# A hybrid attention and convolution trunk on one core: hi parts of late weight chunks cast from memory, their splits moved, a third partial-sum buffer

## The chip, the cores and the metric

The kernel runs on one core of one Trainium2 chip. The metric is device time in microseconds (us) of one execution. Before the change it is 522.34 us, the median of 3 runs (521.39 to 524.71).

A core has five engines, each with its own instruction queue worked strictly in order: TensorE (PE) does matmuls and transposes, VectorE (DVE) and ScalarE (ACT) do elementwise work, GpSimd (POOL) does elementwise work on SBUF and issues the DMAs that convert or accumulate, SyncE (SP) issues the plain DMAs. An instruction that waits for a semaphore holds up everything behind it in its engine's queue.

## The reference, cut to what matters

Two residual layers over x of 512 tokens by 1024 channels, in float32.

```python
def fox_moba_layer(x, norm_g, w_in, ..., w_out):          # layer 0
    proj = rms_norm(x, norm_g) @ w_in                     # 1024 x 4104
    ...                                                   # two kinds of attention, 8 heads each
    return x + (mix * jax.nn.silu(gate)) @ w_out

def conformer_conv_layer(x, norm_g, w_in, conv_w, conv_b, ln_g, ln_b, w_out):   # layer 1
    val, glu_gate, z = jnp.split(rms_norm(x, norm_g) @ w_in, 3, axis=-1)
    u = val * jax.nn.sigmoid(glu_gate)
    u = depthwise_causal_conv(u, conv_w, width=31) + conv_b
    u = jax.nn.silu(layer_norm(u, ln_g, ln_b)) * jax.nn.silu(z)
    return x + u @ w_out
```

The change lies in layer 1, and in how its weights are brought in.

## The kernel before, in words

**Weights.** All weights come as 36 chunks of 1024 rows by 256 columns (two of layer 0 by 260; 1 MB each; 0 to 15 are layer 0's input projection, 16 to 19 its output projection, 20 to 27 the GLU's value and gate columns in turn, 28 to 31 the z columns, 32 to 35 layer 1's output projection). A matmul is made as three products of rounded parts: hi*hi, hi*lo and lo*hi, where hi is the value rounded to the fp32r format and lo the rest. So each chunk is **split**: `load_w` (L152, issued by SP) loads it into a staging tile `wst`, of which there are two; `split_w` makes hi and lo. For chunks from 20 on, lo is made by ACT (L175: minus the rounded chunk) followed by a DMA that POOL issues and that adds the staged chunk onto it (L179). For the chunks in `CAST` (22, 26, 27, 28, 30, 31, 33, 34, 35) hi is made by a DMA that POOL issues and that converts the staged chunk (L169); for the others ACT does it (L173). Chunk 32 alone has its hi cast from memory (L1051) and its lo made by L160 and L161. A staging tile is free, and the load of the chunk after next can start, when the DMA of L179 has landed. hi and lo live in rings: `main` (whi and wlo, two each) or `wx` (four tiles, two chunks). `ahead(n)` traces all splits below n that have not been traced yet.

**Layer 1.** For each of 8 channel tiles ct (128 channels) `glu` makes u; the convolution's 31 taps are shared: DVE adds some of them up in a PSUM accumulator (L766), ACT multiplies the others into one of six `tm` tiles (L775; its first goes straight into the partial sum, L772), and POOL adds those to the partial sum `pacc` (L776). `conv_final` (L783, DVE) joins both sums, `conv_out` transposes the result on PE (L796), takes its statistics on DVE (L798) and puts it back by token on ACT (L799, `ctok`). `pacc` has two buffers, so a tile's ACT and POOL taps can begin when the tile two before it has been transposed. Tiles 6 and 7 are done in two halves of 256 tokens. The first half's taps of both are traced together, then `z_chunk` for chunks 28 to 30, with a split after each.

**The stretch that is written out.** From `conv_out(6, ...)` on, the order on PE, DVE, ACT and POOL is the order of the code (`manual_schedule`); elsewhere a scheduler sets it. The first half goes: transposes of tile 6, the z matmuls of tile 6, transposes of tile 7, most of the z matmuls of tile 7; `norm_stats(0)` (layer norm: variance on DVE, L904, its power of minus a half on POOL, L905, called lnr); `norm_cols` (L911, DVE); transposes back to channels (`ng_t`, L922); then, for four pairs p of channel tiles, `ng_s` (swish, ACT, L928, in the tiles `c`), `ng_m` (times z, DVE, L933), `ng_u` (hi, ACT, L936), `ng_l` (lo, DVE, L939), and the matmuls of four output units with chunks 33 and 34 (L361). The second half's taps of tiles 6 and 7 are put between these by the tables AQ (ACT and POOL) and DQ (DVE). After them the units of chunk 32 and 35 follow, with the second half's transposes between, and at last the same for the second half of the tokens.

Of the kernel before, what the change touches and what calls it, by code (L numbers as in the profile page):

```python
# [9 lines left out]
F32 = mybir.dt.float32  # L10
# [4 lines left out]
ALU = mybir.AluOpType  # L15
# [34 lines left out]
Z6 = 8  # L50
ZK = 6
AQ = (4, 0, 7, 1, 0, 1, 2, 1, 3, 3, 2, 1, 6, 0)
DQ = (3, 5, 2, 0, 0, 2, 2, 2, 4, 3, 3, 5, 99)
# [20 lines left out]
NLATE = 2  # L74
CB = 3
LATE1 = 0
# [18 lines left out]
def tile_kernel(ctx: ExitStack, tc: tile.TileContext, x, xt, w, small0, small1, l1_norm, out):  # L95
# [59 lines left out]
    def split_w(w, ring, eng, parts, cast):  # L155
        st, n = w
        if ring == "late":
# [10 lines left out]
        if cast:  # L168
            G.dma_start(hi, st)  # L169
        for k in range(0, KC, m):  # L170
# [56 lines left out]
    def fetch(i):  # L227
        if i < len(wsrc):
            raw[i] = load_w(*wsrc[i], 4 if i == 0 else 1)

# [517 lines left out]
    def conv_steps(ct, acc, pacc, n0, n):  # L748
# [20 lines left out]
        def astep(i):  # L769
            v, w = tap(i)  # L770
            if i == nv:
                A.activation(pacc[:, o], v, AF.Copy, scale=w)  # L772
                return
            tm = l1.tile([P, S], F32, tag="tm", name="tm", bufs=TMB)
            A.activation(tm[:, :n], v, AF.Copy, scale=w)  # L775
            G.tensor_tensor(pacc[:, o], pacc[:, o], tm[:, :n], op=ALU.add)  # L776

# [24 lines left out]
    def new_pacc():  # L802
        return l1.tile([P, S], F32, tag="pacc", name="pacc", bufs=2)

# [109 lines left out]

    pts_, cs_ = {}, {}

# [8 lines left out]
    def ng_s(h, k):  # L925
        pt = pts_[h, k // 2]
        c = cs_[h, k] = l1.tile([P, HT], F32, tag="c", name="c", bufs=CB)
        A.activation(c, pt[:, (k % 2) * HT:(k % 2 + 1) * HT], AF.Silu, bias=lnb[:, k:k + 1],  # L928
                     scale=lng[:, k:k + 1])
# [26 lines left out]
    for i in range(max(len(v6), len(v7) + LAG)):  # L956
        j = i - LAG
        for f in v6[i:i + 1] + (v7[j:j + 1] if j >= 0 else []):
            f()
    for i in range(max(len(a6), len(a7) + LAGA)):  # L960
        j = i - LAGA
        for f in a6[i:i + 1] + (a7[j:j + 1] if j >= 0 else []):
            f()
    for ct in late:
        conv_final(*ends[ct], 0, HT)()
    for c in range(3):
        z_chunk(28 + c, c)
        ahead(34 + c)

# [43 lines left out]
    with tc.manual_schedule(engines=engs):  # L1013
# [19 lines left out]
        for p in range(4):  # L1033
# [21 lines left out]
            for (c, t), po in zip(units, banks):  # L1055
                out1_mm(c, t, po, (2 * p, 2 * p + 1))
        for (c, t), po in zip(units, banks):
            out1_add(c, t, po)
# [129 lines left out]
```

## Time and profile before

| | before |
|---|---|
| median of 3 runs | 522.34 us |
| the profiled execution's own time | 522.39 us |
| its span, first to last instruction | 520.6 us |
| PE busy | 503.7 us, 97% |
| DVE, ACT, POOL busy | 373.0, 329.1, 232.6 us |
| mean granted TensorE clock | 0.996 |

The profiled execution took 0.05 us more than the median, and 1.8 us of its time lie outside the span. The page gives busy time, idle time and what ended it, by engine and line; a matmul's recorded time includes its way through the array, so that records overlap, and a PE that is busy all the time is seen from its start times. The granted clock of 1.00 is 2.4 GHz and 0.50 is 1.2 GHz. DMA share is the mean busy share of the core's 16 DMA engines.

### The profile page before, as it was taken

Reading aid. Unit: us, or ns where it says so; the run is one execution under the profiler, and the core shown is the slowest. Engines: PE = TensorE matmul, PEld = TensorE weight load, DVE = VectorE, ACT = ScalarE, POOL = GpSimd, SP = SyncE. Lnnn points to the kernel's source line nnn. Section 1 sums busy time; section 2 is a strip of 40 time slices with the busy share of each in tenths; the row PEclk is TensorE's granted clock in tenths of the full one; section 3 lists DMA queues with packets and bytes.
Section 4 is the critical chain, followed back from the end, with each engine's and each line's share of the span. In section 5 each row is a group of like instructions: output and inputs, shape, how many; then the busy total and the mean of one; then the engine's idle time right before and its main releaser. Section 6 shows DMA issues by size and latency. Waiting matters only on the chain.

```text
span 520.6 us, 9754 instructions
## 1 busy us (share of the span) xinstructions
PE 503.7 (97%) x3694; PEld 459.9 (88%) x3694; DVE 373.0 (72%) x788; ACT 329.1 (63%) x668; POOL 232.6 (45%) x255
## 2 busy tenths in 40 slices
PE   8999999999999999999999999999999999769997
PEld 4999998987889988788789999999999888548997
DVE  7745677676465577596685256999999997868741
ACT  4945678777645775576384735998676765377230
POOL 5264852020422233223101113879988985687200
PEclk9999999999999999999999999999999999989999
DMA  8742222302122242402219668488999799962111
GB/s 293 318 145 81 84 81 83 102 24 83 61 102 94 82 111 99 144 14 108 102 52 395 130 205 242 82 211 286 235 306 259 212 270 305 262 170 105 41 51 42
DMA packets 16566, 79.05 MB, mean 152 GB/s; under 512 B 1988, under 2 KB 4352, under 8 KB 8712
## 3 DMA queue, kind: packets, MB, share of 16 engines
q1 hardware_dynamic: 12632, 51.08, 27.1%
q0 software_dynamic: 3744, 27.26, 22.0%
q8 instruction: 29, 0.48, 0.4%
q10 hardware_dynamic: 144, 0.09, 0.1%
q14 instruction: 17, 0.14, 0.1%
HBM read 50.07 MB, written 2.14 MB: 100 GB/s over the span
## 4 chain that ended last, share of the span: by engine, by line
PE 70%; DMA 8%; POOL 7%; ACT 6%; DVE 4%; issue 3%; SPq 0%; POOLq 0%; ACTq 0%
PE mm L361 29%; POOL pacc L776 6%; PE mm L370 6%; PE mm L371 6%; PE mm L372 6%; DMA wst<-in_w_dram 5%; PE st L361 4%; PE o L603 3%; PE tp L526 3%; PE o L361 2%; PE s L510 2%; PE s L512 2%; DMA wlo<-wst 1%; DMA xt<-in_xt_dram 1%; PE s L361 1%
## 5 line engine op out<-in xcount | busy, mean ns | idle before, releaser
L776 POOL TENSOR_TENSOR pacc<-pacc,tm 128x256 f32<-128x256 f32 (+1 forms) x125 | 120.7, 986 | 15.8 <-ACT tm L775 10.1
L766 DVE SCALAR_TENSOR_TENSOR s<-u,parts,s 128x256 f32<-128x256 f32 (+1 forms) x211 | 108.1, 569 | 0.5
L361 PE MATMUL mm<-wlo,hhi 128*128 128x256 f32 (+1 forms) x352 | 98.7, 287 | 0.8 <-DVE wlo L177 0.5
L361 PE MATMUL mm<-whi,hhi 128*128 128x256 f32 (+1 forms) x352 | 98.4, 287 | 0.0
L361 PE MATMUL mm<-whi,hlo 128*128 128x256 f32 (+1 forms) x352 | 98.3, 286 | 0.0
L775 ACT ACTIVATE tm<-u,parts 128x256 f32<-128x256 f32 (+1 forms) x125 | 66.2, 571 | 14.5 <-POOL pacc L776 14.0
L361 PEld LDWEIGHTS mm<-wlo,hhi 128*128 128x128 f32 x352 | 65.8, 190 | 2.0 <-DVE wlo L177 0.8
L361 PEld LDWEIGHTS mm<-whi,hhi 128*128 128x128 f32 x352 | 65.6, 189 | 0.7 <-issue 0.2
L361 PEld LDWEIGHTS mm<-whi,hlo 128*128 128x128 f32 x352 | 65.9, 190 | 0.2
L177 POOL TENSOR_TENSOR wlo<-wst,whi 128x512 fp32r<-128x512 f32 (+1 forms) x22 | 31.0, 1423 | 57.4 <-ACT whi L173 57.4
L173 ACT ACTIVATE whi<-wst 128x512 fp32r<-128x512 f32 (+2 forms) x77 | 49.4, 707 | 5.9 <-DMA wst<-in_w_dram 2.7
L518 POOL TENSOR_TENSOR cb<-cb,mask 128x128 f32<-128x128 f32 x32 | 15.5, 490 | 80.7 <-DVE nm L522 46.2
L523 ACT ACTIVATE p<-p,nm 128x128 f32<-128x128 f32 (+3 forms) x64 | 35.7, 559 | 24.1 <-DVE nm L522 23.6
L177 DVE TENSOR_TENSOR wlo<-wst,whi 128x512 fp32r<-128x512 f32 (+1 forms) x50 | 39.8, 830 | 9.0 <-PE o L361 7.1
L370 PE MATMUL mm<-nhi,wx 128*128 128x256 f32 (+1 forms) x104 | 33.0, 318 | 0.0
L371 PE MATMUL mm<-nlo,wx 128*128 128x256 f32 (+1 forms) x104 | 32.2, 309 | 0.0
L372 PE MATMUL mm<-nhi,wx 128*128 128x256 f32 (+1 forms) x104 | 31.9, 307 | 0.0
L371 PE MATMUL mm<-nlo,whi 128*128 128x256 f32 (+1 forms) x104 | 31.8, 307 | 0.0
L372 PE MATMUL mm<-nhi,wlo 128*128 128x256 f32 (+1 forms) x104 | 31.7, 306 | 0.0
L370 PE MATMUL mm<-nhi,whi 128*128 128x256 f32 (+1 forms) x104 | 31.7, 307 | 0.0
L526 PE MATMUL tp<-identf,p 128*128 128x128 f32 x160 | 28.4, 275 | 1.1 <-ACT p L523 0.7
L396 POOL TENSOR_TENSOR rq<-vq,mhalf 128x16 f32<-128x16 f32 x8 | 26.2, 3272 | 6.2 <-DVE vq L394 6.1
(292 smaller groups left out, 1436.3 us busy)
## 6 DMA issues: line engine op xcount, KB each, us to landing
wst<-in_w_dram SPq DMA_DIRECT2D x33, 1024.0 KB, 5.0
wx<-wst POOLq DMA_DIRECT2D x13, 1024.0 KB, 7.2
wlo<-wst POOLq DMA_DIRECT2D x8, 1024.0 KB, 8.4
whi<-wst POOLq DMA_DIRECT2D x3, 1024.0 KB, 4.5
wst<-in_w_dram SPq DMA_DIRECT2D x2, 1040.0 KB
xs<-in_x_dram SPq DMA_DIRECT2D x4, 512.0 KB, 10.3
cb<-cdram SPq DMA_DIRECT2D x8, 256.0 KB, 3.5
x<-in_x_dram SPq DMA_DIRECT2D x4, 512.0 KB, 6.5
```

Source lines behind the costliest of these rows:

```text
L173: A.activation(hi[:, ks], st[:, ks], AF.Copy)
L177: (V if eng is G and parts == 4 and k % 4 and V0 else eng).tensor_tensor(lo[:, ks], st[:, ks], hi[:, ks].bitcast(F32), op=ALU.subtract)
L361: T.matmul(po, a[:, k, ts], b[:, k, :n], start=first and i == 0, stop=last and i == len(prods) - 1)
L370: T.matmul(po, whi[:, k, cs], a, start=k == 0, stop=False)
L371: T.matmul(po, whi[:, k, cs], b, start=False, stop=False)
L372: T.matmul(po, wlo[:, k, cs], a, start=False, stop=k == KC - 1)
L396: G.tensor_tensor(r, v, mhalf[:, :16].rearrange("p (t h) -> p t h", t=NT), op=ALU.pow)
L523: A.activation(p[:, :w], p[:, :w], AF.Exp, bias=nm, scale=-1.0, accum_out=sm[:, h, t:t + 1])
L526: T.transpose(tp[:, j * P:(j + 1) * P], p[:, j * P:(j + 1) * P], identf)
L766: V.scalar_tensor_tensor(acc[:, o], v, w, first[0][:, :n] if i == 1 else acc[:, o], op0=ALU.mult, op1=ALU.add)
L775: A.activation(tm[:, :n], v, AF.Copy, scale=w)
L776: G.tensor_tensor(pacc[:, o], pacc[:, o], tm[:, :n], op=ALU.add)
```

## The change

It does four things.

1. The casting DMA of L169 reads the chunk from memory in place of the staging tile. The staging tile is still loaded, since lo is made of it. The DMA count and the bytes written stay; for nine chunks the source is another.
2. The splits of chunks 33 and 34 are no longer traced after the z chunks 28 and 29 alone: `issue_after` puts ACT's instructions of the split behind the 9th (33) and 17th (34) step of the list of first-half taps of tiles 6 and 7, and POOL's behind that step's addition. The split of chunk 35 moves out of the z loop into the written-out stretch, after the output matmuls of pair p = 1.
3. `pacc` has three buffers.
4. The three `c` tiles of the swish become two tiles of a pair each, in the ring `sg`.

```diff
--- before.py
+++ after.py
@@ -49,6 +49,7 @@
 FB = 1
 Z6 = 8
 ZK = 6
+TW = (8, 16)
 AQ = (4, 0, 7, 1, 0, 1, 2, 1, 3, 3, 2, 1, 6, 0)
 DQ = (3, 5, 2, 0, 0, 2, 2, 2, 4, 3, 3, 5, 99)
 C34 = 0
@@ -72,7 +73,6 @@
 STK = 1
 PTS = 3 * P
 NLATE = 2
-CB = 3
 LATE1 = 0
 LATE2 = 1
 SIX = 2
@@ -153,7 +153,7 @@
         return st, n
 
     def split_w(w, ring, eng, parts, cast):
-        st, n = w
+        (st, n), src = w
         if ring == "late":
             lo = l1p[0].tile([P, KC * WC], F32R, tag="gh", name="lo", bufs=1)
             lo = lo.rearrange("p (k n) -> p k n", k=KC)
@@ -166,7 +166,7 @@
             hi, lo = (flat(l1p[0], F32R, "wx", n, 4, WC) for _ in range(2))
         m = KC // parts
         if cast:
-            G.dma_start(hi, st)
+            G.dma_start(hi.rearrange("p k n -> p (k n)"), w_ap(*src, 0, KC))
         for k in range(0, KC, m):
             ks = slice(k, k + m)
             if not cast:
@@ -226,7 +226,7 @@
 
     def fetch(i):
         if i < len(wsrc):
-            raw[i] = load_w(*wsrc[i], 4 if i == 0 else 1)
+            raw[i] = load_w(*wsrc[i], 4 if i == 0 else 1), wsrc[i]
 
     def split(i):
         if i < len(wsrc):
@@ -772,8 +772,8 @@
                 A.activation(pacc[:, o], v, AF.Copy, scale=w)
                 return
             tm = l1.tile([P, S], F32, tag="tm", name="tm", bufs=TMB)
-            A.activation(tm[:, :n], v, AF.Copy, scale=w)
-            G.tensor_tensor(pacc[:, o], pacc[:, o], tm[:, :n], op=ALU.add)
+            return (A.activation(tm[:, :n], v, AF.Copy, scale=w),
+                    G.tensor_tensor(pacc[:, o], pacc[:, o], tm[:, :n], op=ALU.add))
 
         return ([partial(vstep, i) for i in range(nv)],
                 [partial(astep, i) for i in range(nv, CONV)])
@@ -800,7 +800,7 @@
                      pt[:, t0 * P:(t0 + n) * P].rearrange("p (t c) -> p t c", t=n), AF.Copy)
 
     def new_pacc():
-        return l1.tile([P, S], F32, tag="pacc", name="pacc", bufs=2)
+        return l1.tile([P, S], F32, tag="pacc", name="pacc", bufs=3)
 
     nf, nsp = [18], [17]
 
@@ -912,7 +912,7 @@
                             op0=ALU.subtract, op1=ALU.mult)
 
 
-    pts_, cs_ = {}, {}
+    pts_, cs_, cp = {}, {}, [None]
 
     def ng_t(h, p):
         pt = pts_[h, p] = tpbank()
@@ -924,7 +924,9 @@
 
     def ng_s(h, k):
         pt = pts_[h, k // 2]
-        c = cs_[h, k] = l1.tile([P, HT], F32, tag="c", name="c", bufs=CB)
+        if k % 2 == 0:
+            cp[0] = l1.tile([P, 2, HT], F32, tag="sg", name="c", bufs=2)
+        c = cs_[h, k] = cp[0][:, k % 2]
         A.activation(c, pt[:, (k % 2) * HT:(k % 2 + 1) * HT], AF.Silu, bias=lnb[:, k:k + 1],
                      scale=lng[:, k:k + 1])
 
@@ -957,15 +959,19 @@
         j = i - LAG
         for f in v6[i:i + 1] + (v7[j:j + 1] if j >= 0 else []):
             f()
+    taps = []
     for i in range(max(len(a6), len(a7) + LAGA)):
         j = i - LAGA
         for f in a6[i:i + 1] + (a7[j:j + 1] if j >= 0 else []):
-            f()
+            taps.append(f())
     for ct in late:
         conv_final(*ends[ct], 0, HT)()
+
     for c in range(3):
         z_chunk(28 + c, c)
-        ahead(34 + c)
+        if c < 2:
+            with tc.issue_after(taps[TW[c]][0].ins), tc.issue_after(taps[TW[c]][1].ins):
+                ahead(34 + c)
 
     (v6, a6), (v7, a7) = (conv_steps(ct, *ends[ct], HT, HT) for ct in late)
     vsteps = v6[:V6]
@@ -1054,6 +1060,8 @@
                 ng_t(0, p + 1)
             for (c, t), po in zip(units, banks):
                 out1_mm(c, t, po, (2 * p, 2 * p + 1))
+            if p == 1:
+                ahead(36)
         for (c, t), po in zip(units, banks):
             out1_add(c, t, po)
         ca(99)
```

What moves is seen in three places. The first is POOL's queue around the splits of chunks 33 and 34, where pacc_5225 is tile 6's partial sum and pacc_5227 tile 7's. Before:

```order
L776 TENSOR_TENSOR pacc_5225<-pacc_5225,tm_5288 128x256
L169 DMA whi_5387<-wst_5231 128x2048
L776 TENSOR_TENSOR pacc_5225<-pacc_5225,tm_5294 128x256
L179 DMA wlo_5388<-wst_5231 128x2048
L169 DMA whi_5446<-wst_5392 128x2048
L776 TENSOR_TENSOR pacc_5225<-pacc_5225,tm_5300 128x256
L179 DMA wlo_5447<-wst_5392 128x2048
L776 TENSOR_TENSOR pacc_5225<-pacc_5225,tm_5306 128x256
L776 TENSOR_TENSOR pacc_5225<-pacc_5225,tm_5312 128x256
L776 TENSOR_TENSOR pacc_5227<-pacc_5227,tm_5291 128x256
L776 TENSOR_TENSOR pacc_5225<-pacc_5225,tm_5318 128x256
L776 TENSOR_TENSOR pacc_5227<-pacc_5227,tm_5297 128x256
```

And now (chunk 33's cast, L169, stands two rows above the first of these):

```order
L776 TENSOR_TENSOR pacc_5225<-pacc_5225,tm_5294 128x256
L776 TENSOR_TENSOR pacc_5227<-pacc_5227,tm_5303 128x256
L776 TENSOR_TENSOR pacc_5225<-pacc_5225,tm_5300 128x256
L179 DMA wlo_5388<-wst_5231 128x2048
L776 TENSOR_TENSOR pacc_5227<-pacc_5227,tm_5309 128x256
L776 TENSOR_TENSOR pacc_5225<-pacc_5225,tm_5306 128x256
L776 TENSOR_TENSOR pacc_5227<-pacc_5227,tm_5315 128x256
L776 TENSOR_TENSOR pacc_5225<-pacc_5225,tm_5312 128x256
L776 TENSOR_TENSOR pacc_5227<-pacc_5227,tm_5321 128x256
L169 DMA whi_5446<-in_w_dram 128x2048
L179 DMA wlo_5447<-wst_5392 128x2048
L776 TENSOR_TENSOR pacc_5225<-pacc_5225,tm_5318 128x256
```

Tile 7's additions, which all came after tile 6's eighth, now alternate with tile 6's; each L169 names the memory as its source; tile 6's last addition (tm_5318) stands behind chunk 34's L179 in both, in the fourth row behind it before and in the first now.

The second is POOL's queue around the first lnr (the upper L905), up to the second. Before:

```order
L776 TENSOR_TENSOR pacc<-pacc,tm 128x256 x14
L169 DMA wx<-wst 128x2048
L776 TENSOR_TENSOR pacc<-pacc,tm 128x256
L179 DMA wx<-wst 128x2048
L905 TENSOR_TENSOR lnr<-lnv,mhalf 128x2
L776 TENSOR_TENSOR pacc<-pacc,tm 128x256 x8
L1051 DMA hi<-in_w_dram 128x2048
L776 TENSOR_TENSOR pacc<-pacc,tm 128x256 x18
L905 TENSOR_TENSOR lnr<-lnv,mhalf 128x2
```

And now:

```order
L776 TENSOR_TENSOR pacc<-pacc,tm 128x256 x7
L905 TENSOR_TENSOR lnr<-lnv,mhalf 128x2
L776 TENSOR_TENSOR pacc<-pacc,tm 128x256 x8
L1057 DMA hi<-in_w_dram 128x2048
L776 TENSOR_TENSOR pacc<-pacc,tm 128x256 x3
L169 DMA wx<-in_w_dram 128x2048
L179 DMA wx<-wst 128x2048
L776 TENSOR_TENSOR pacc<-pacc,tm 128x256 x15
L905 TENSOR_TENSOR lnr<-lnv,mhalf 128x2
```

Chunk 35's two DMAs, which stood one and three rows ahead of lnr, stand behind lnr, eleven additions and chunk 32's cast.

The third is ACT's queue in the written-out stretch, from the z swish of tile 7 on to pair p = 2. Before:

```order
L1007 ACTIVATE zs<-mm 128x512
L928 ACTIVATE c<-tp,parts 128x256 x2
L775 ACTIVATE tm<-u_3251,parts 128x256
L936 ACTIVATE u_5510<-c 128x256 x2
L775 ACTIVATE tm<-u_3251,parts 128x256 x2
L928 ACTIVATE c<-tp,parts 128x256 x2
L775 ACTIVATE tm<-u_3251,parts 128x256
L936 ACTIVATE u_5510<-c 128x256 x2
```

And now:

```order
L1013 ACTIVATE zs<-mm 128x512
L930 ACTIVATE c<-tp,parts 128x256 x2
L775 ACTIVATE tm<-u_3251,parts 128x256
L938 ACTIVATE u_5505<-c 128x256 x2
L775 ACTIVATE tm<-u_3251,parts 128x256 x2
L175 ACTIVATE wx<-wst 128x2048
L930 ACTIVATE c<-tp,parts 128x256 x2
L775 ACTIVATE tm<-u_3251,parts 128x256
L938 ACTIVATE u_5505<-c 128x256 x2
```

Chunk 35's copy (L175, 2048 elements wide) stands between pair 1's hi parts and pair 2's swish. Before, it stood ahead of tile 7's `ctok` copy, before the first lnr was used.

## Rows read from the trace of the kernel before

**Rows 1.** The page: its first line.

```profile
span 520.6 us, 9754 instructions
```

**Rows 2.** The table of stretches: from and to in us of the span, length, then busy time and instructions of PE, PEld, DVE, ACT and POOL, granted clock, DMA share, GB/s. The last row is a stretch of 2 us.

```profile
420.00:430.00 10.00, 10.00 (x48) 8.20 (x47) 10.00 (x23) 6.38 (x14) 9.45 (x10) 1.00 1.04 210
430.00:440.00 10.00, 10.00 (x47) 8.18 (x46) 9.52 (x26) 5.53 (x7) 4.37 (x7) 1.00 0.94 342
440.00:450.00 10.00, 8.53 (x39) 6.60 (x37) 6.14 (x16) 7.00 (x16) 9.25 (x13) 1.00 1.06 261
450.00:460.00 10.00, 4.84 (x22) 3.47 (x20) 5.37 (x15) 4.47 (x8) 5.15 (x8) 1.00 0.78 250
460.00:470.00 10.00, 8.49 (x46) 7.12 (x47) 9.29 (x18) 6.42 (x17) 8.46 (x12) 0.83 0.68 161
470.00:480.00 10.00, 9.12 (x75) 8.65 (x74) 8.38 (x20) 9.39 (x24) 7.57 (x11) 1.00 0.14 52
480.00:490.00 10.00, 9.92 (x84) 9.56 (x83) 8.40 (x24) 1.18 (x3) 5.09 (x7) 1.00 0.20 67
...
462.00:464.00 2.00, 2.00 (x8) 1.74 (x7) 2.00 (x6) 1.42 (x3) 1.84 (x3) 0.50 0.96 197
```

**Rows 3.** The timeline of PE: start in us, length in us, line and operation, out<-in, shape, count, and in brackets the idle time before and what ended it. The transposes of tiles 6 and 7, the last z matmul before the normalized values are transposed, the first of those transposes, and the first output matmul.

```profile
444.35 0.44 PE L796 MATMUL tp<-identf,pacc 128*128 128x128 f32 x2 [1.48 <-DVE pacc L783]
...
452.04 0.41 PE L796 MATMUL tp<-identf,pacc 128*128 128x128 f32 x2 [1.74 <-DVE pacc L783]
...
456.18 0.40 PE L372 MATMUL mm<-nhi,wx 128*128 128x512 f32 x1
460.50 0.30 PE L922 MATMUL tp<-identf,ctok 128*128 128x128 f32 x1 [3.92 <-DVE ctok L911]
...
465.53 0.38 PE L361 MATMUL st<-whi,u 128*128 128x256 f32 x1 [0.28 <-ACT u L936]
```

**Rows 4.** The chain of waits that ended last, between 426 and 463 us: start, length, what.

```profile
426.86 7.53 DMA wst<-in_w_dram
...
434.47 1.93 ACT wlo L175
...
436.68 7.72 DMA wlo<-wst
...
444.53 10.91 DMA wst<-in_w_dram
...
455.53 1.91 ACT wx L175
...
457.74 0.87 POOL wx L179
458.61 0.76 POOL lnr L905
...
459.40 1.83 DVE ctok L911 x2
...
461.27 1.68 PE tp L922 x7
```

**Rows 5.** The timeline of POOL: start, length, instruction, count, idle time before.

```profile
421.08 9.50 POOL L776 TENSOR_TENSOR pacc<-pacc,tm 128x512 f32<-128x512 f32 x9
434.93 0.60 POOL L169 DMA_DIRECT2D whi<-wst  x1 [4.34 <-DMA wst<-in_w_dram]
...
442.43 9.13 POOL L776 TENSOR_TENSOR pacc<-pacc,tm 128x256 f32<-128x256 f32 x12 [0.20 <-ACT pacc L772]
456.02 0.60 POOL L169 DMA_DIRECT2D wx<-wst  x1 [4.47 <-DMA wst<-in_w_dram]
...
459.06 7.47 POOL L776 TENSOR_TENSOR pacc<-pacc,tm 128x256 f32<-128x256 f32 x8
```

**Rows 6.** The timeline of DVE, in the same columns.

```profile
438.15 2.04 DVE L766 SCALAR_TENSOR_TENSOR s<-u,parts,s 128x256 f32<-128x256 f32 x5
443.87 0.42 DVE L783 TENSOR_TENSOR pacc<-s,pacc 128x256 f32<-128x256 f32 x1 [3.68 <-POOL pacc L776]
...
451.46 0.42 DVE L783 TENSOR_TENSOR pacc<-s,pacc 128x256 f32<-128x256 f32 x1
...
453.52 0.17 DVE L904 TENSOR_SCALAR lnv<-mv 128x2 f32<-128x2 f32 x1
...
463.65 1.29 DVE L933 TENSOR_TENSOR c<-c,zs 128x256 f32<-128x256 f32 x2
```

**Rows 7.** The timeline of ACT, in the same columns.

```profile
441.85 0.49 ACT L772 ACTIVATE pacc<-u,parts 128x256 f32<-128x256 f32 x1
...
465.06 0.72 ACT L936 ACTIVATE u<-c 128x256 fp32r<-128x256 f32 x2 [1.51 <-PE mm L371]
...
469.90 1.02 ACT L928 ACTIVATE c<-tp,parts 128x256 f32<-128x256 f32 x2 [0.92 <-PE tp L922]
```

**Rows 8.** DMAs: from the list of DMA issues (count, KB each, median us to landing) the casts of staged chunks into whi and the cast from memory; from the view of L179 between 400 and 465 us the least, median and greatest us to landing; and a row of the table of stretches in which two loads from memory were under way.

```profile
whi<-wst POOLq DMA_DIRECT2D x3, 1024.0 KB, 4.5
...
hi<-in_w_dram POOLq DMA_DIRECT2D x1, 1024.0 KB, 5.1
...
DMA to landing us min/median/max: 7.7/9.7/14.7
...
282.00:284.00 2.00, 2.00 (x19) 2.00 (x18) 0.44 (x2) 0.66 (x4) 0.00 (x0) 1.00 1.04 436
```

## The prediction

> **What bounds the kernel now.** I read the table of stretches first, to see where PE, the engine that is busy nearly all the time, is not. From 420 to 440 us it never stops, and from 480 us hardly; between 440 and 480 us it idles 1.47 + 5.16 + 1.51 + 0.88 = 9.0 us, and in 462 to 464 us it runs at a granted clock of 0.50, which is 1.2 GHz, right after its longest idle time [rows 2]. Whatever is won in this stretch is kept to the end, since PE is full behind it. The timeline of PE gives the gaps: 1.48 us before the transposes of tile 6, 1.74 us before those of tile 7, 3.92 us before the transposes of the normalized values (L922) [rows 3].
>
> The chain of waits tells what the longest hung on: chunk 33's load, its copy on ACT, its accumulating DMA, then chunk 35's load into the freed staging tile, its copy, its accumulating DMA on POOL, and only then lnr, `ctok` and the transposes [rows 4]. In the data lnr does not need chunk 35; it stands behind it in POOL's queue. POOL waited 4.47 us at chunk 35's cast [rows 5]. lnv was ready at 453.52 + 0.17 = 453.69 us [rows 6], and lnr began at 458.61 [rows 4]: 4.9 us late.
>
> The two smaller gaps: DVE was through with its share of tile 6 at 438.15 + 2.04 = 440.19 us and waited 3.68 us for POOL's sum [rows 6], and POOL had itself stood 4.34 us at chunk 33's cast, waiting for its load [rows 5]. From tile 6's final sum (443.87) to tile 7's (451.46) DVE works without a break, 7.59 us [rows 6]; the second gap is its.
>
> **The change, part by part.** *Casts from memory.* Their number stays. A cast of a staged chunk lands in 4.5 us, the one from memory in 5.1 us [rows 8]. Nobody waits for hi alone: chunk 33's cast went out at 434.93 and its first reader is the output matmul at 465.53 [rows 5, 3]. I take 0; without that cover it would be 0.6 us a cast. What the edit does not remove is the load: lo is still made of the staging tile, so POOL's L179 waits for ACT's copy, and that for the load.
>
> One rule speaks against a second read from memory. Two loads from memory moved 436 GB/s together [rows 8]. The Trainium skill (DMA: Bandwidth & Descriptors, section Where 436 GB/s comes from) puts transfers between memory and SBUF at about 358 GB/s for a core and those inside SBUF at 435. By that a 1 MB cast would take some 0.5 us longer (an estimate from the page's figures), and the two casts near chunk 33's load would make 518.3 us of my sum; the row is against it.
>
> *Splits of 33 and 34, with the third pacc buffer.* Chunk 33's load ends as before, at 426.86 + 7.53 = 434.4, its copy at 436.4, and L179 goes out at 436.68 [rows 4]. POOL's wait at L169 thus becomes a wait at L179, of about the same length, with tile 6's remaining additions queued behind it and DVE waiting for them. What changes is how many are left: nine half-tile additions stand ahead of this L179 instead of five. Tile 7's can, because its first tap no longer waits until 441.85 for a buffer [rows 7]. An addition takes 9.13 / 12 = 0.76 us [rows 5], an issue 0.6. From 436.68: the issue 0.6, five additions 3.8, chunk 34's cast and L179 1.2, tile 6's last addition 0.8, so 443.1 against 443.87, 0.8 us sooner. I keep 0.5, since chunk 33's cast now runs beside its load. The bounds: 3.7 us sooner, where DVE's own work sets the final sum (440.19), and 2.5 us later, where the load shares its time with half of a 5.1 us cast. I take the value nearest to the unchanged row of the load. For tile 7 the extra buffer buys nothing more: POOL is through at 443.1 + 3 x 0.76 = 445.4, and DVE asks 7.59 us after tile 6.
>
> *Chunk 35 behind lnr.* All with the 0.5: lnv is ready at 453.2, lnr takes 0.76 [rows 4], `ctok` starts at 454.0. PE comes to L922 when its z matmuls end, at 456.18 + 0.40 - 0.5 = 456.1 instead of 460.50 [rows 3]; the first normalized tile is done by then (a pair takes 1.83 [rows 4]). Next, hi needs DVE's product with z: before, the first of the pair ended at 463.65 + 0.65 = 464.3, 4.9 us after `ctok` began at 459.40 [rows 6, 4]; now 458.9. ACT waited past that for PE's last z matmul, till 465.06 [rows 7], which the low clock had stretched; at the full clock six z matmuls of 0.24 us (24 and two transposes fill the 5.95 us from 444.35 to the gap before 452.04 [rows 3]) and eight transposes of 0.12 (seven took 1.68 at the low clock [rows 4]) end by 456.1 + 2.4 = 458.5. The first output matmul follows 0.47 us after hi begins [rows 7, 3]: 459.4 against 465.53, **6.1 us** won. If the clock fell as before, the 4.75 us from 460.50 to the end of the z matmuls would come back, and 4.7 us would be won.
>
> *Chunk 35's copy in the written-out stretch.* 1.91 us on ACT [rows 4] go between pair 1's hi and pair 2's swish, where ACT idled 0.92 us [rows 7]: **1.0 us** lost, since in 470 to 480 us ACT is busy 9.39 of 10 [rows 2] and PE's pairs follow it. Bounds 0 and 1.9. Load 35 should be there: even at 444.53 + 10.91 = 455.4 [rows 4], as before, it precedes the copy's turn, which is 469.90 - 0.92 - 465.06 = 3.9 us after the first hi [rows 7]: 462.8. POOL's two issues for it fall where POOL waits for that copy or for taps; 0, and at most 1.5 us if the second half's last sum is late by both (0.60 + 0.87 [rows 5, 4]), as PE has only 0.08 us free in 480 to 490 [rows 2]. Chunk 34's accumulating DMA, out at about 442, lands by 457 even at the slowest 14.7 us [rows 8], before its first use near 461. The pair tiles for c relax waits that held nobody: 0.
>
> **Sum.** 522.39 (the profiled execution, span 520.6 [rows 1] and 1.8 around it) - 6.1 + 1.0 = **517.3 us**. The median lies 0.05 us below that execution, so nothing is shifted for it.
>
> **Rivals.** *A, load 33 late.* DMA share is 1.04 in 420 to 430 us, at only 210 GB/s [rows 2]; the cast, moved ahead, joins a full queue. Tile 6's sum then comes 2.5 us later than before instead of 0.5 sooner, and everything with it: 517.3 + 3.0 = 520.3. Against it: the cast's work was there before, only later, beside chunk 34's load. The Trainium skill (same page, section Issuing engines are not separate DMA queues) says that DMAs of all issuing engines share the same 16 DMA engines and interleave, which is this rival; the share above 1 agrees.
>
> *B, POOL is no longer late at all.* If load 33 lands 3 us earlier (casts no longer touch the staging tiles, the queue ahead of it is rearranged), DVE sets tile 6: 3.2 us more, 514.1. For it speaks that every load in this chain starts when an accumulating DMA lands, and those took 7.7 to 14.7 us [rows 8]; against it, that PE's hold on the wx ring, which starts the chain, is unchanged.
>
> *C, slower.* ACT stands at chunk 35's copy in the written-out stretch with swish, hi and all later taps queued behind it. Load 35 starts when chunk 33's accumulating DMA lands. By the slowest rows, 436.7 + 14.7 + 10.9 = 462.3 [rows 8, 4], it is just in time at 462.8. Each us after that is a us of the kernel; the gain is gone at 468, and at 473.5 the time is 528. Only a load 11 us beyond the slowest rows gets there.
>
> **Chances.** Forecast 0.48 (its own range 515.3 to 519.3), A 0.25, B 0.20, C 0.05, none of them 0.02. 1% is 5.2 us (517.1 to 527.6), about what a measurement of this kernel can tell from no change. Faster by over 1%: B and a little under half of the forecast, 0.42; within: 0.52; slower: 0.06. The range runs from 513.5 (B with part of the copy's cost gone) to 521.5 (A with the clock falling once more).
>
> **What would show it.** POOL's lnr follows DVE's lnv within 0.2 us; the gap before L922 is under 1 us; the granted clock stays at 1.00 in the 10 us in which it averaged 0.83. POOL shows a wait of 3 to 5 us at L179 for ACT's wlo, with no L169 waiting for a load. DVE still waits some 3 us at L783 for POOL, and PE still has gaps of about 1 and 1.7 us before L796. ACT's L175 stands ahead of pair 2's swish with no wait for its load. A wait there of more than 1 us, or a DVE wait at L783 above 5 us, would break the sum; none at L783 would mean B.

## The result: 0.8% slower, and the profile after

The changed kernel took 526.54 us (median), the kernel before 522.1 in the same rounds: 1.0079 times as long, 95% interval 1.0051 to 1.0107. That is above the predicted 517.3 and above the range's end of 521.5, though within 1%. Medians, here and below, are of all executions, while the ratios are of means and leave out those over 1.5% above the fastest of their kernel (here one of 696.77 us; the others took 524.62 to 529.23). The profiled execution is the fastest one, 524.62 us; [rows 1] had 520.6 of span.

```profile
span 522.9 us, 9739 instructions
```

The table of stretches of the changed kernel, columns as in [rows 2]:

```profile
410.00:420.00 10.00, 4.80 (x40) 4.37 (x38) 10.00 (x13) 2.93 (x6) 5.98 (x6) 0.97 0.77 211
420.00:430.00 10.00, 9.97 (x31) 7.93 (x32) 10.00 (x13) 6.86 (x9) 6.45 (x7) 0.69 0.90 220
...
440.00:450.00 10.00, 10.00 (x47) 8.15 (x46) 9.96 (x28) 7.23 (x12) 8.43 (x12) 1.00 1.01 264
450.00:460.00 10.00, 10.00 (x47) 8.14 (x46) 8.10 (x23) 4.24 (x11) 3.41 (x6) 1.00 1.00 274
460.00:470.00 10.00, 7.79 (x38) 6.21 (x37) 9.75 (x20) 7.51 (x19) 7.93 (x11) 0.86 0.18 53
470.00:480.00 10.00, 9.12 (x73) 8.66 (x72) 7.95 (x20) 9.62 (x21) 7.88 (x11) 0.97 0.86 224
...
420.00:426.00 6.00, 5.97 (x14) 4.71 (x15) 6.00 (x10) 5.87 (x7) 3.50 (x5) 0.50 0.75 214
```

The same stretch of the kernel before, which the prediction had not looked at, and a tap of DVE ahead of it:

```profile
410.00:420.00 10.00, 10.00 (x63) 8.95 (x62) 10.00 (x14) 7.30 (x9) 7.74 (x7) 1.00 0.71 239
...
406.52 0.68 DVE L763 TENSOR_SCALAR first<-u,parts 128x256 f32<-128x256 f32 x1
```

Of the 9.0 us of idle PE in 440 to 480 us, 0 + 0 + 2.21 + 0.88 = 3.1 are left: 5.9 us won. But PE now idles 5.2 us in 410 to 420, where it never stopped, and then runs at a granted clock of 0.50, 1.2 GHz, up to 426. The time that a low clock costs, length times what is missing of 1.00, was 1.7 us in 410 to 480 before; it is 0.3 + 3.1 + 1.4 + 0.3 = 5.1 now. In sum -5.9 + 5.2 + 3.4 = +2.7 us, and the span grew by 2.3. The timeline of four engines tells what the new idle time hangs on:

```profile
406.92 0.91 POOL L179 DMA_DIRECT2D wx<-wst  x1
407.54 6.57 POOL L776 TENSOR_TENSOR pacc<-pacc,tm 128x512 f32<-128x512 f32 x5
408.80 5.46 DVE L763 TENSOR_SCALAR first<-u,parts 128x256 f32<-128x256 f32 x1
...
416.16 0.88 DVE L798 BATCH_NORM_STATS2 stats<-tp 128x6 f32<-128x128 f32 x4
417.07 0.60 ACT L799 ACTIVATE ctok<-tp 128x512 f32<-128x512 f32 x1 [7.17 <-DVE stats L798]
419.40 0.58 ACT L744 ACTIVATE sg<-st 128x512 f32<-128x512 f32 x1
420.03 0.80 PE L370 MATMUL st<-nhi,whi 128*128 128x512 f32 x1 [5.23 <-ACT sg L744]
```

One first tap on DVE takes 5.46 us, eight times the 0.68 that the same one took before at 406.52. It is tile 6's: its shape is 128x256, and of the late tiles only 6 and 7 are done in halves of 256 tokens. (The expectations below call it tile 5's.) It ends at 414.26, with POOL's run of five additions (414.11). Behind it in DVE's order stand three more taps and the statistics of tile 3; ACT waits for these, with the gate's sigmoid (L744) behind them in its queue; and PE waits for the sigmoid, which reads the PSUM tile st that PE is to write. In POOL's order these five additions now go by turns to tile 4's and tile 5's partial sums; with two buffers tile 5 had none yet, and POOL added tile 4's alone, with gaps.

The end of the stretch:

```profile
457.39 0.38 PE L796 MATMUL tp<-identf,pacc 128*128 128x128 f32 x2
461.83 0.30 PE L922 MATMUL tp<-identf,ctok 128*128 128x128 f32 x1
465.99 0.39 PE L361 MATMUL st<-whi,u 128*128 128x256 f32 x1 [1.00 <-ACT u L938]
...
469.83 1.91 ACT L175 ACTIVATE wx<-wst 128x2048 fp32r<-128x2048 f32 x1
```

Before the transposes of tiles 6 and 7 there is no gap (451.60 for tile 6), and none before the normalized values', where [rows 3] had 1.48, 1.74 and 3.92 us. The last is as forecast: lnr begins at 459.08, right after lnv (458.84 + 0.17), and chunk 35's copy waits for no load. The other two are not: the sums come later than before (tile 6's at 448.96 against 443.87), and PE comes later still. For the same reason DVE waits for POOL at neither L783, which the prediction had named as a sign of rival B, without B's gain. Tile 6's transposes begin 7.3 us and tile 7's 5.4 us later than before, so that L922 starts 1.3 us later and the first output matmul 0.5.

### The profile page after: what moved, and what is told of

It is laid out like the page before. It is cut to its first block, busy times and chain, and to the rows that moved or that the text cites. A ratio compares the mean times of both kernels' runs of the same rounds, so it can differ in the third digit from the quotient of the medians.

```text
span 522.9 us, 9739 instructions
## 1 busy us (share of the span) xinstructions
PE 506.3 (97%) x3694; PEld 462.3 (88%) x3694; DVE 380.3 (73%) x788; ACT 327.6 (63%) x668; POOL 231.1 (44%) x255
## 4 chain that ended last, share of the span: by engine, by line
PE 71%; DVE 17%; ACT 4%; POOL 2%; issue 2%; DMA 2%; SPq 0%; POOLq 0%; ACTq 0%; DVEq 0%
PE mm L361 29%; DVE s L766 9%; PE mm L370 6%; PE mm L371 6%; PE mm L372 6%; PE st L361 4%; PE o L603 3%; PE tp L526 3%; DVE first L763 2%; PE o L361 2%; POOL pacc L776 2%; PE s L510 2%; PE s L512 2%; DMA xt<-in_xt_dram 1%; PE st L370 1%
## 5 line engine op out<-in xcount | busy, mean ns | idle before, releaser
L775 ACT ACTIVATE tm<-u,parts 128x256 f32<-128x256 f32 (+1 forms) x125 | 64.5, 570 | 5.5 <-POOL pacc L776 5.3
```

What stands on the lines that cost most here:

```text
L775: return (A.activation(tm[:, :n], v, AF.Copy, scale=w), G.tensor_tensor(pacc[:, o], pacc[:, o], tm[:, :n], op=ALU.add))
```

## The experiments

Theory H (hold): POOL's additions, freed by the third buffer, hold up a DVE tap in 404 to 415 us. Against it stood that the casts from memory delay the loads, or that the moved splits do the harm. The first four kernels each undo or do one part.

**Two buffers again** (in the changed kernel):

```diff
-        return l1.tile([P, S], F32, tag="pacc", name="pacc", bufs=3)
+        return l1.tile([P, S], F32, tag="pacc", name="pacc", bufs=2)
```

> The changed kernel with two partial-sum buffers again; casts from memory, moved splits and the pair tiles stay. Theory (the third buffer lets POOL add five taps without a gap, and DVE's first tap of tile 5, from SBUF to SBUF, takes 5.46 us instead of 0.68 beside them, so that the statistics of tile 3, ACT's copy L799, the gate L744 of tile 7 and the matmuls come late): the 5.46 us and the matmuls' 5.2 us wait for L744 near 415 are gone, the clock of 420 to 430 is back near 1.00, and the time is 515 to 519 us. Rival, the casts from memory: 525 to 527. Rival, the moved splits: 525 to 527.

Measured 526.6 us, 1.0065 (1.0043 to 1.0086). This goes against H, which had 515 to 519; the third buffer is not all that makes the change slow. Its profile comes further down.

**Buffer and pair tiles alone, in the kernel before** (`bufs=3`, and L927 as in the change):

> The kernel before with the third partial-sum buffer alone (and the pair tiles that make room for it). Theory of the third buffer: the late first tap and the 5 us wait of the matmuls near 415 are here too, and the gain of chunk 35's move is not: 526 to 532 us. Rivals (casts, moved splits): 521 to 523, with the first tap of tile 5 under 1.5 us.

528.23 us, 1.0103 (1.0082 to 1.0125). The buffer alone does harm. Its profile (of its fastest execution, 525.96 us) shows another way than H: no tap is held, tile 6's first one having begun at 404.93, ahead of POOL's run by turns (408.67); POOL's queue has tile 7's additions among tile 6's, and PE waits 5.2 us for tile 6's final sum (448.39 instead of 443.87, [rows 6]).

```profile
448.87 0.69 PE L796 MATMUL tp<-identf,pacc 128*128 128x128 f32 x2 [5.25 <-DVE pacc L783]
```

**Casts from the staging tile again** (in the changed kernel, `G.dma_start(hi, st)`):

> The changed kernel with the casts from the raw tile in SBUF again; third buffer and moved splits stay. Theory of the third buffer: the wait near 415 stays, 525.5 to 527 us. Rival, the casts: the wait is gone, 515 to 519.

526.48 us, 1.0066 (1.0045 to 1.0086). A tap of 8.40 us at 406.25, PE stalled as in the change. So H's stall does not need the casts from memory.

**First taps into PSUM** (in the changed kernel; the arithmetic is the same):

```diff
-                V.tensor_scalar(first[0][:, :n], v, w, cbias[:, ct:ct + 1], op0=ALU.mult,
+                V.tensor_scalar(acc[:, o], v, w, cbias[:, ct:ct + 1], op0=ALU.mult,
...
-                V.scalar_tensor_tensor(acc[:, o], v, w, first[0][:, :n] if i == 1 else acc[:, o],
+                V.scalar_tensor_tensor(acc[:, o], v, w, acc[:, o],
```

> The changed kernel with every tile's first tap written to its bank in PSUM instead of to an SBUF tile, so that DVE has no tap with both sides in SBUF and none with two inputs in SBUF. The scheduler's order changes a little with it (unit 28 of the z branch before unit 29). Theory (DVE is held up beside POOL's additions only where both use SBUF twice): third buffer kept, no tap of DVE over 1.5 us, the matmuls' wait for L744 under 1.5 us, 514 to 518 us. If the first tap is late for a reason of its own (its data, or its place): still 5 us, 525 to 527.

522.49 us, 0.9992 (0.9977 to 1.0007): 4 us come back, less than the 514 to 518 us expected. PE is full from 400 to 440 at a clock of 1.00. What is then next on the path is the prediction's rival A, in the timeline of this kernel:

```profile
428.13 0.80 POOL L169 DMA_DIRECT2D whi<-in_w_dram  x1
438.50 1.92 ACT L175 ACTIVATE wlo<-wst 128x2048 fp32r<-128x2048 f32 x1 [9.53 <-DMA wst<-in_w_dram]
447.74 0.69 PE L795 MATMUL tp<-identf,pacc 128*128 128x128 f32 x2 [4.92 <-DVE pacc L782]
```

Chunk 33's load lands at about 438.5, 4 us later than before, and tile 6's sum comes late by that.

**Chunk 35's split alone, in the kernel before:**

```diff
-        ahead(34 + c)
+        if c < 2:
+            ahead(34 + c)
...
+            if p == 1:
+                ahead(36)
```

> The kernel before with one part of the change: the split of chunk 35 behind the second pair of the output stage, so behind lnr; casts, two buffers and the splits of 33 and 34 as before. If the prediction's third step is right in itself (POOL stood at chunk 35's cast for 4.5 us with lnr behind it), lnr follows lnv within 0.3 us, the first transposes L922 come about 4 us sooner (456 to 457 instead of 460.5) and the time is 516 to 519 us. If what lnr gains is lost again behind it (chunk 35 late, the clock), the time is 521 to 523.

**518.91 us, 0.9925 (0.9907 to 0.9944)**: the best kernel of the study, faster than both. Its timeline:

```profile
453.28 0.72 POOL L905 TENSOR_TENSOR lnr<-lnv,mhalf 128x2 f32<-128x2 f32 x1 [1.41 <-DVE lnv L904]
455.31 3.19 DVE L911 TENSOR_SCALAR ctok<-ctok,mv,lnr 128x512 f32<-128x512 f32 x4
456.03 0.30 PE L922 MATMUL tp<-identf,ctok 128*128 128x128 f32 x1
460.18 0.39 PE L361 MATMUL st<-whi,u 128*128 128x256 f32 x1 [1.00 <-ACT u L936]
465.84 1.01 ACT L928 ACTIVATE c<-tp,parts 128x256 f32<-128x256 f32 x2
```

The first output matmul comes 465.53 - 460.18 = 5.35 us sooner, pair 2's swish 469.90 - 465.84 = 4.06: the copy costs 1.3, and the span is 4.1 shorter (516.5).

**All three splits moved, in the kernel before** (chunk 35 as above, 33 and 34 as in the change's `issue_after` lines):

> The kernel before with all of the moved splits (33 and 34 held behind taps, 35 behind lnr) and nothing else: two buffers, casts from the raw tile. POOL ends tile 6's additions ahead of chunk 33 here, and has chunks 33 and 34 between tile 7's. Theory (with two buffers, the splits among tile 7's taps make tile 7's sum late, as the version of the change with two buffers measured 526.6): 524 to 528 us, the wait for tile 7's sum is what grew. Rival (that version was slow by its casts): 515 to 520.

523.78 us, 1.0023 (1.0008 to 1.0039): the move of 33 and 34 costs 4.9 us against the kernel just above. Its timeline:

```profile
442.20 1.90 ACT L175 ACTIVATE wlo<-wst 128x2048 fp32r<-128x2048 f32 x1
444.48 0.50 ACT L772 ACTIVATE pacc<-u,parts 128x256 f32<-128x256 f32 x1
445.06 1.61 POOL L776 TENSOR_TENSOR pacc<-pacc,tm 128x256 f32<-128x256 f32 x2 [3.30 <-ACT pacc L772]
...
456.85 0.42 DVE L783 TENSOR_TENSOR pacc<-s,pacc 128x256 f32<-128x256 f32 x1 [7.49 <-POOL pacc L776]
457.42 0.66 PE L796 MATMUL tp<-identf,pacc 128*128 128x128 f32 x2 [8.00 <-DVE pacc L783]
```

Tile 6's final sum comes at 441.79, 2.1 us sooner than in [rows 6]. But the copy of chunk 34 stands on ACT ahead of tile 7's first tap (L772), which starts at 444.48 instead of 441.85 [rows 7]; and POOL's four issues for chunks 33 and 34 (0.59 + 0.90 + 0.59 + 0.89 us), which before were over by 440.63, now stand among tile 7's additions. POOL finishes tile 7 only at 456.8. All this is with two buffers; what the move does with three is told below.

**All casts from memory, nothing else, in the kernel before:**

```diff
-            G.dma_start(hi, st)
+            G.dma_start(hi.rearrange("p k n -> p (k n)"), w_ap(*src, 0, KC))
```

> The kernel before with the casts from memory alone. POOL has chunk 33's cast earlier now and both of its accumulations L179 one or two additions later. Theory (a cast from memory that no longer waits for its load runs beside that load, and takes from it): load 33 lands 1.5 to 2.5 us later, tile 6's sum too, 522 to 525 us. Prediction's first step (casts cost nothing): 521.5 to 522.5.

526.23 us, 1.0057 (1.0034 to 1.0079): 3.0 us by the ratio, 3.8 between the medians. The list of DMA issues between 355 and 420 us (queue, count, KB each, median us to landing):

```profile
wst<-in_w_dram SPq DMA_DIRECT2D x6, 1024.0 KB, 5.5
wx<-in_w_dram POOLq DMA_DIRECT2D x4, 1024.0 KB, 6.0
wx<-wst POOLq DMA_DIRECT2D x4, 1024.0 KB, 12.0
wlo<-wst POOLq DMA_DIRECT2D x2, 1024.0 KB, 11.0
...
DMA to landing us min/median/max: 10.3/11.6/14.6
```

and the kernel before (the last row of both is of the six accumulating DMAs of L179 alone):

```profile
wst<-in_w_dram SPq DMA_DIRECT2D x6, 1024.0 KB, 5.3
wlo<-wst POOLq DMA_DIRECT2D x2, 1024.0 KB, 8.1
...
DMA to landing us min/median/max: 7.7/8.6/13.3
```

The loads themselves take hardly longer; the accumulating DMAs take 11.6 instead of 8.6 us at the median. Each of them frees a staging tile, so the next load starts late: the second one of the stretch at 376.07 instead of 372.42, chunk 33's at 429.29 instead of 426.86. On the path this is a wait of ACT for chunk 32's load and the rest of the chain behind it:

```profile
425.65 1.92 ACT L160 ACTIVATE lo<-wst 128x2048 fp32r<-128x2048 f32 x1 [8.14 <-DMA wst<-in_w_dram]
437.72 0.69 DVE L783 TENSOR_TENSOR pacc<-s,pacc 128x512 f32<-128x512 f32 x1 [6.41 <-POOL pacc L776]
```

**Two buffers again, with a profile:**

> The changed kernel with two buffers once more, for a profile at full clock. Expected with 526.6 us: tile 6's sum in time (transposes of tile 6 not waiting), the first tap of tile 5 under 1.5 us, and the growth in tile 7's sum or in the raw loads of 33 and 34. If instead tile 5's first tap is late again, the additions without a gap are not the third buffer's doing.

526.7 us, 1.0057 (1.0035 to 1.008). No tap over 1.56 us from 400 us on, and still slow: ACT waits 7.12 us for chunk 32's load, as with the casts alone, and PE 2.23 us for tile 6 and 8.34 for tile 7, as with the moved splits. That tile 6 was late too was not expected. So with two buffers it is the casts and the moved splits that cost what chunk 35 wins.

The next four ask for what holds the tap, and size the casts. **Blocks behind the finished output:** 24 blocks, each with a run of POOL additions to one accumulator and one DVE tap beside it; they add work and leave the output alone.

> The kernel before with a measurement added behind its last output: 24 small blocks, in each of which ACT releases a run of 0, 1, 2, 3, 5 or 8 additions 128x512 on POOL (SBUF to SBUF, back to back) and at the same time one operation on PSUM on DVE, behind which DVE has the operation measured: a first tap from SBUF to SBUF, a tap with two inputs in SBUF, a first tap from SBUF to PSUM, a tap with its sum in PSUM. The added work leaves the output as it is and makes the run longer. Theory (a DVE operation that uses SBUF on both sides waits until POOL's whole run is over, not only its present addition): the first two kinds take 0.7 us without additions, and grow with the run, by about 1.1 to 1.3 us for each addition, to 5 us and more at 5; the last two kinds stay under 1 us. Rival (it waits for one addition at most): no kind over 2 us at any length. Rival (the 5.46 us came from something else, such as ACT's or the DMAs' use of SBUF): all kinds under 1 us.

A tap from SBUF to SBUF took 0.54 us alone and 1.12 to 1.15 beside POOL, with one addition or eight; one with two SBUF inputs 0.74 and 1.19; with PSUM as the output, or as an input, 0.81 and 0.75 always. So POOL's run as such does not hold a tap to its end.

**Only tile 5's first tap into PSUM** (in the changed kernel, `first.append(acc[:, o] if ct == 5 else ...)`):

> The changed kernel with tile 5's first tap alone written to PSUM; the casts, the third buffer, the moved splits and nearly all of the order stay. If this one tap of 5.46 us is what makes the matmuls wait near 415: that wait goes, and the time comes to that of the version with all first taps in PSUM, 522 to 524 us. If the late loads make up for it: no matmul wait near 415, but 525.5 to 527 all the same. If the tap was not the cause: the wait stays.

Six of the twelve times lie from 519.66 to 527.05 us, the other six from 527.52 to 531.23; the median of all is 527.29, and the ratio of 0.9991 (0.9957 to 1.0024) leaves the upper six out. The profile (528.3):

```profile
405.77 0.81 DVE L764 TENSOR_SCALAR s<-u,parts 128x512 f32<-128x512 f32 x1
406.48 6.94 DVE L764 TENSOR_SCALAR first<-u,parts 128x256 f32<-128x256 f32 x1
```

Tile 5's first tap, now in PSUM, takes 0.81 us. The tap behind it, of 128x256, is tile 6's: the one held in the change, still written to SBUF here, and held again. So this kernel left the tap that matters as it was, and says nothing on whether that one alone is the cause.

**Casts of chunks 26 and 27 alone from memory** (in the kernel before):

> The kernel before with the casts of chunks 26 and 27 alone from memory; no instruction stands in another place. Theory (two raw tiles in a ring: a load that starts late makes every later load late, so one stretch where the casts from memory and the loads share the reading pays for all): the load that started at 372.42 starts about 3 us later, those of chunks 30 to 32 too, and the time is 524 to 526.5 us, most of what all nine casts cost. Rival (each cast costs by itself, and the order of chunks 33 and 34 did the rest): 521.5 to 523.

523.41 us, 1.0013 (0.9992 to 1.0033), less than expected. The next load starts 3.3 us later, those after it 1.6, 1.6, 1.9, 0.3 and 0.4: the delay dies out where later casts stay local. The cost of the casts does not come from these two alone.

**Chunk 35 and first taps in PSUM, in the kernel before:**

> The kernel before with chunk 35's split behind lnr, and all first taps in PSUM. If DVE's taps beside POOL's additions (1.2 and 1.9 us instead of 0.5 to 0.7 in the kernel before) are on the path: 515.5 to 518 us, below the 518.9 of the move alone. If DVE has room there, or the bank that a first tap now needs holds it up: 518.5 to 521.

520.13 us, 0.994 (0.9916 to 0.9964): no gain over 518.91 with two buffers.

**The blocks, with additions by turns to two accumulators:**

> The same measurement behind the output, with one thing changed: POOL's additions go by turns to two accumulators, as they do in the changed kernel between tiles 4 and 5, instead of all to one (where each waits for the one before it); the first four blocks keep one accumulator for comparison. Theory (between additions that wait for each other DVE gets in, between independent ones it does not): the first tap from SBUF to SBUF and the tap with two inputs in SBUF take about 1.2 us beside five additions on one accumulator, and 4 to 6 us beside five by turns, 8 to 10 beside eight; the two kinds with PSUM stay under 1 us. Rival (the long taps came from another cause): all under 1.5 us again.

No tap over 1.26 us: turns alone don't hold it.

**The best kernel with the third buffer** (and the pair tiles):

> The kernel before with chunk 35's split behind lnr, and the third buffer. Theory (the third buffer does harm by itself, by mixing tile 7's additions in among tile 6's and by additions of POOL that leave DVE no gap): 523 to 526 us, 4 to 6 above the move of chunk 35 alone. Rival (the third buffer did harm only together with the late chunk 35): 517 to 520.

526.49 us, 1.0071 (1.0048 to 1.0094): the buffer costs 7.6 us here. Its timeline:

```profile
406.88 8.44 DVE L766 SCALAR_TENSOR_TENSOR s<-u,parts,first 128x512 f32<-128x512 f32 x1
407.58 0.91 POOL L179 DMA_DIRECT2D wx<-wst  x1
408.19 6.57 POOL L776 TENSOR_TENSOR pacc<-pacc,tm 128x512 f32<-128x512 f32 x5
...
423.02 0.79 PE L370 MATMUL st<-nhi,whi 128*128 128x512 f32 x1 [7.57 <-ACT sg L744]
```

**The same with first taps in PSUM:**

> The same with all first taps in PSUM, so that DVE has no tap that POOL's additions hold up. If the gap-free additions were all that is wrong with the third buffer: 515 to 519 us. If the mixing of the tiles and the wait for chunk 33's load are worth as much: 520 to 524.

520.27 us, 0.9948 (0.9922 to 0.9974), PE without the stall. The held tap is 6.2 of the buffer's 7.6 us, and the buffer gains nothing (520.13 with two buffers and the same taps).

**First taps in PSUM and casts from staging** (in the changed kernel):

> The changed kernel with all first taps in PSUM, and the casts from the raw tile again; third buffer and all moved splits stay. The version with the casts from memory and the first taps in PSUM measured 522.5, with ACT waiting 9.5 us for chunk 33's raw load. Theory (the casts from memory are what makes the loads late there): ACT waits 5 to 7 us for that load, tile 6's sum comes 2 to 4 us sooner, 517.5 to 520.5 us. Rival (the loads are as late without them): 521.5 to 523.5.

519.53 us, 0.993 (0.9905 to 0.9955): 3.0 us less than with the casts from memory. Chunk 33's load still makes ACT wait 5.10 us, as before the change (5.29). This kernel differs from the one just above in the move of chunks 33 and 34 alone: 519.53 against 520.27, with intervals that overlap. With first taps in SBUF the same pair is 526.48 (casts from the staging tile again) against 526.49 (the best kernel with the third buffer). So with three buffers the move costs nothing that can be told from noise.

**The blocks, with ACT making the additions' operands as in the kernel:**

> The measurement behind the output once more, now with ACT making each of POOL's second operands in a ring of six tiles at the same time, as in the kernel; eight additions a block, on one accumulator in the first six blocks and on two by turns in the last six; the measured operation of DVE comes behind two or four operations with their sum in PSUM. Theory (POOL keeps DVE out only while ACT feeds it operands ahead, with additions on two accumulators): first taps from SBUF to SBUF of 4 us and more in the blocks by turns, under 2 us in the others. Rival (something else in the kernel, which no block behind the output has, such as DMAs or TensorE): all under 1.5 us again, and the cause of the long taps stays open.

All taps at most 1.83 us. Two of POOL's additions by turns:

```profile
592.48 1.26 POOL L1131 TENSOR_TENSOR paccb<-paccb,tm 128x512 f32<-128x512 f32 x1
593.70 1.27 POOL L1131 TENSOR_TENSOR pacc<-pacc,tm 128x512 f32<-128x512 f32 x1
```

**The same, with POOL issuing a 1 MB accumulating DMA behind the second addition:**

> The measurement behind the output with the last part of the kernel's surroundings that it lacked: behind the second of eight additions POOL issues a transfer with accumulation of 1 MB between two SBUF tiles that are no longer needed, as it does for a weight chunk; ACT feeds the additions as before; additions on one accumulator in the first eight blocks, on two by turns in the last eight; the measured first tap (SBUF to SBUF, or two inputs in SBUF) comes at four different places of the run. Theory (POOL's issue of a transfer, or the transfer itself, together with additions by turns, keeps DVE out until the run ends): some first taps of 4 us and more in the blocks by turns, behind the issue. Rival: all under 2 us again; then it stays open what makes them long in the changed kernel.

The hold is there. One block of this kernel with additions by turns:

```profile
642.65 0.88 POOL L1137 DMA_DIRECT2D zs<-ctok  x1
643.26 1.56 POOL L1135 TENSOR_TENSOR pacc<-pacc,tm 128x512 f32<-128x512 f32 x1
644.48 1.55 POOL L1135 TENSOR_TENSOR paccb<-paccb,tm 128x512 f32<-128x512 f32 x1
...
643.45 7.72 DVE L1142 TENSOR_SCALAR first<-u,parts 128x512 f32<-128x512 f32 x1
```

Three more taps that begin behind such an issue take 5.35 to 7.52 us, each to the end of POOL's run; those that begin ahead of the issue, or 0.01 us after its start, at most 1.73. With one accumulator behind an issue the longest is 2.49. The additions by turns start 1.22 us apart and take about 1.55, so each begins 0.3 us before the one ahead has ended; on one accumulator each waits for the last. In the blocks without the issue they start as far apart and take 1.26, an overlap of 0.04 us. Behind the issue the additions thus overlap more; that this is what keeps the tap out is a guess that no run tests.

## Why the prediction was wrong

**The third buffer: the sentence that failed is "for tile 7 the extra buffer buys nothing more".** The sum put the buffer at nothing, by looking for what it does from 434 us on. The buffer belongs to every tile: ACT's first tap (L772) of tiles 2 to 5 comes 7.6, 7.3, 10.3 and 17.0 us sooner in the change (tile 5's at 391.67 instead of 408.71), and among the additions so freed are tile 5's at 404 to 414. There they close the gaps of POOL's run, and a DVE tap is held through all of it: 5.46 us, then PE's 5.2 us, then the low clock. With chunk 35 moved and nothing else, the buffer takes the time from 518.91 to 526.49 us, which is the time of the whole change (526.54); 6.2 of these 7.6 us go when first taps write PSUM.

**Chunk 35 behind lnr: right.** The waits named are gone: lnr follows lnv, the gap before L922 closes. Done alone it won 5.35 us at the first output matmul, where 6.1 was forecast, 0.5 of it by the splits: `ctok` began at 455.31, not 454.5 (454.0 with these 0.5), since DVE was at taps when lnr came. The copy cost 1.3, inside its bounds of 0 to 1.9 (taken: 1.0). That is 4.1 us of the profiled span (3.9 by the ratio, 522.45 x 0.0075) against 5.1, or 4.6 without the splits' share. Done alone, the granted clock stayed at 1.00 in 450 to 470 us; rival C occurred neither there nor in the change.

**Casts from memory at nothing: wrong.** "Nobody waits for hi alone" is true and beside the point. The cast shares its time with the accumulating DMAs, which take 11.6 instead of 8.6 us at the median, and each of these frees a staging tile for a load. Alone they cost 3.0 to 3.8 us; out of the changed kernel with its taps in PSUM, 3.0. Rival A had the mechanism, but for one chunk; it runs through all late chunks. The Trainium skill (DMA: Bandwidth & Descriptors, section Where 436 GB/s comes from) had spoken against the term; by it 1 us was lost, and three to four were. This fits its direction; that it is the limit on memory reads is not shown, since the loads got hardly longer (5.5 against 5.3 us) and the accumulations did.

**The splits of 33 and 34: nothing with the third buffer, 4.9 us without.** The prediction had them together with the buffer, for 0.5 us won; with three buffers the two pairs of kernels show 0.0 and 0.7 us won, which noise covers. With two buffers tile 6 came sooner, as said (2.1 us), but tile 7 lost 5.4 us (457.42 against 452.04): chunk 34's copy of 1.9 us on ACT stands ahead of the tap that opens tile 7's partial sum, and the four issues on POOL stand among its additions. With three buffers that tap comes long before the copies (431.46 against 439.16 and 444.12 in the change). The working did not count the copies on ACT; the buffer covered it.

**They don't add.** With two buffers they do: 518.9 for chunk 35, 4.9 for the splits and 3.0 to 3.8 for the casts make 526.8 to 527.6, and 526.6 was measured. With three, the buffer alone already gives 526.5, and splits and casts add nothing to it. They take the same slack: when PE has lost 8 us at 410 to 426, loads, copies and tile 7 have that long to catch up. Chunk 33's copy waits 2.13 us for its load in the change (at 439.16), and 9.53 us without the held tap. The changed kernel goes from 526.5 to 522.5 without the held tap, to 519.5 without the casts from memory too, against 518.9 for chunk 35 alone.

Two smaller readings were off and change nothing of this: an issue of L179 takes 0.87 us, not 0.6, so that tile 6's sum works out at 443.6 and not 443.1; and with the clock falling as before, 456.1 instead of 460.50 leaves 4.4 us won, not 4.7.

## What to carry to other kernels

Take a change of several parts apart before believing any one price: here one small edit was worth 3.9 us and the others took back more. When a buffer is added, look at the first place in the program where its engine runs ahead, not at the place it was meant for, and ask what the fuller queue collides with. When a step is moved, count its instructions on every engine.

## What the runs showed of the hardware

A DVE tap can be held for a whole run of POOL instructions, not one: 5.35 to 8.44 us in the rows above. In the blocks it took three things together: a POOL run by turns on two accumulators, a DMA issued by POOL in it, and a tap that reads and writes SBUF alone, or has two SBUF inputs. With PSUM as output or accumulator no hold was seen. The Trainium skill (SBUF — State Buffer, section SBUF: two separate sides) says that a DVE operation in a two-port mode, or with two SBUF inputs, and a GpSimd operation share a port pair: the one that starts first has it for its whole instruction, and the other waits. The two SBUF inputs agree with the rows; that the first tap from SBUF to SBUF runs in such a mode is not shown (it takes 0.54 us alone, and 0.81 with PSUM as its output). The length of the wait is more than one instruction, since five or six additions passed before the tap ended. The changed kernel has it twice more, 4.03 us at 364.53, and here:

```profile
425.37 0.88 POOL L161 DMA_DIRECT2D lo<-wst  x1
425.98 2.97 POOL L776 TENSOR_TENSOR pacc<-pacc,tm 128x256 f32<-128x256 f32 x3
426.05 3.21 DVE L766 SCALAR_TENSOR_TENSOR s<-u,parts,first 128x256 f32<-128x256 f32 x1
```

Why the issue is needed stays open, and whether it must come ahead of the tap: in the blocks it did, but the tap of 8.44 us began 0.7 us ahead of L179. Open too is why the times of the kernel with only tile 5's tap in PSUM spread over 11.6 us.
